# Second attention layer: query blocks take 3 to 9 ticks by their width, and low parts of the probabilities meet only V's high columns

## The chip, the cores and the metric

The kernel runs on one core of one Trainium2 chip. The metric is the device time of one execution in microseconds (us). Three runs of the kernel before took 1335.98, 1336.43 and 1338.58 us; the median is 1336.43.

## What is computed

Two layers over a sequence of 1024 tokens, width 1024, float32. Layer A is chunked attention with 16 heads of 64 and a learned bias. Then one shared K and V is projected from the stream. Layer B is differential attention against it: 8 heads, each with two softmax maps, the second subtracted from the first with a learned factor. Only layer B's attention is changed:

```python
s = jnp.einsum('bhmqd,bhmkd->bhmqk', qblk, k).astype(jnp.float32) * scale
qchunk = (bi * Q_BLOCK + jnp.arange(Q_BLOCK)) // CHUNK
mask = kchunk[None, :] <= qchunk[:, None]
s = jnp.where(mask[None, None, None], s, NEG_INF)
p = jax.nn.softmax(s, axis=-1)
a = p[:, :, 0] - lam * p[:, :, 1]
return jnp.einsum('bhqk,bhkd->bhqd', a.astype(v.dtype), v)
...
o = rmsnorm(o, b_subln[j]) * (1.0 - lam_init)
y = (o.reshape(B, S, B_WIDTH) * jax.nn.silu(g)) @ b_w_out[j]
```

The mask is causal, so query block i (128 tokens, i = 0 to 7) needs the key blocks 0 to i: its scores are 128 x 128(i + 1).

## The kernel before

**Numbers.** Every float32 operand of a matrix product is kept as a high and a low part (`hi_of` on ScalarE, L189, and `lo_of` on VectorE, L192), and a product is the sum of high x high, high x low and low x high. V stands as 128 high and 128 low columns side by side, so a matmul of a block of probabilities against it has 256 output columns; the two halves are added afterwards (L972 and L948).

**Order by ticks.** The class `Ticks` writes the program in the order in which the engines get it. In a tick come first the tensor operations registered for it with `K.at`, then four matmuls of a filler (the projections of the layer, a stream of 128x512 matmuls, L232 to L236), then what `K.after` and `K.later` registered for the other engines, by rank and then by the order of registering. Nothing is reordered at run time: each engine takes its instructions in that order and waits for what each one needs.

**Units.** A unit is one head of layer B: 48 ticks, 192 fillers. In this text the ticks of a unit's attention are counted from its block 0; its tick 48 is tick 0 of the next unit. While a unit's attention runs, the fillers compute its own V and gate projections in the ticks 0 to 23 and then K, Q, K, Q of the next unit (two token halves), six ticks a group; the four K and Q groups end with the ticks 29, 35, 41 and 47.

**A block** of `attB_block` starts at tick t0 with the scores of its first map (L562), and at t1 come those of the second. The scores of both go to one tile `sp` in PSUM, of which the pool `psS` has a single buffer: a matmul of scores waits until VectorE has read the ones before (the reduction, L571, emitted in the tick of the scores). ScalarE's exponential (L577) follows a tick later. Before, t1 = t0 + 3, and a block follows the last after 6 ticks. Counted from t1 the rest stands the same before and after:
- tick t1 + 2: `norm` on GpSimd, two inverses (L169) and a scaling (L901 before, L905 after);
- tick t1 + 3: `mix` on VectorE, which subtracts the second map from the first (L906, then L910);
- tick t1 + 5, for key blocks 4 to 7 also t1 + 6: the transposes of the mixed probabilities (L165), then high and low parts;
- four ticks after the transposes: the matmuls against V (L936, then L941). The block is closed seven ticks later with a transpose of its output (`c5`) and a product on VectorE (`c6`, L967, then L972).

**Rotation of K and Q** (`rope`). When a K or Q group ends, ScalarE copies it (L851), four small DMAs move pieces of it, GpSimd multiplies twice (L857, L858, emitted two and three ticks later), VectorE adds (L859, six ticks later), ScalarE makes the high parts (seven ticks) and VectorE the low parts (L192 on 64 partitions, twice, eight ticks later).

**Weights.** GpSimd scales a weight slice (L207, in the ticks 0, 18, 24 and 42 of a unit's attention), ScalarE makes its high part two ticks later and VectorE its low part (`wlo`) three ticks later.

Of the kernel before, what the change touches and what calls it, by code (L numbers as in the profile page):

```python
# [23 lines left out]
P = 128  # L24
# [27 lines left out]
def bcast_rows(ap, n):  # L52
    """[1, n] DRAM row -> the same row on every partition."""
    return ap.broadcast_to([P, n])


class Ticks:
    """Emission order: every tick issues its tensor work, a few filler matmuls,
    then the work of the other engines that is due."""
# [47 lines left out]
def trunk(ctx, tc, x, positions, a_norm_pre, a_w_in, a_rel_rev, a_w_out, a_norm_post,  # L107
# [27 lines left out]
    # DRAM scratch  # L135
# [8 lines left out]
    # resident operands  # L144
# [37 lines left out]
    def sumsq(src, dump):  # L182
        """row sums of squares; the squares themselves go to dump, which is free."""
        ss = st()
        A.activation(dump, src, AF.Square, accum_out=ss)
        return ss
# [7 lines left out]
    # ---------------------------------------------------------------- weights  # L194
# [17 lines left out]
    class Weights:  # L212
        """slices in the order of use; a slice's load goes out with the split before it."""
# [13 lines left out]
    def mm_group(w, xT):  # L227
        """one [128 cols, 512 tokens] projection, a matmul at a time."""
        hi, lo = w
        acc = acc_tile()  # L230
        for c in range(NC):
            T.matmul(acc, lhsT=hi[:, c, :], rhs=xT(0, c), start=(c == 0), stop=False)  # L232
            yield acc
            T.matmul(acc, lhsT=hi[:, c, :], rhs=xT(1, c), start=False, stop=False)  # L234
            yield acc
            T.matmul(acc, lhsT=lo[:, c, :], rhs=xT(0, c), start=False, stop=(c == NC - 1))  # L236
            yield acc
# [3 lines left out]
    def proj_stream(W, xT, done, slow, quarters=False):  # L241
        """every projection of a layer; kinds k, q, v, g are slices 0..3 of a unit."""
        seq = [(u, kind, half) for u in range(8) for kind, half in ORDER]
        if quarters:
            yield from mm_quarters(W, xT(0), done)
        for n, (u, kind, half) in enumerate(seq):
            if quarters and n < 2:
                continue
            m = 0
            for acc in mm_group(W.cut[4 * u + kind], xT(half)):  # L250
                m += 1
                if m == 2 and n + 1 < len(seq):
                    k = 4 * seq[n + 1][0] + seq[n + 1][1]
                    if k not in W.cut:
                        W.split(k)
                if m == 24:
                    done(u, kind, half, acc)
                yield
                if n >= 61 and m % slow == 0:
                    yield  # L260

    def mm_quarters(W, xT, done):
        """the first two groups, 256 tokens at a time."""
        accs = [acc_tile(), acc_tile()]
        for part in range(2):
            cs = slice(part * 256, part * 256 + 256)
            for kind in range(2):
                hi, lo = W.cut[kind]
                m = 0
                for c in range(NC):  # L270
                    for w, l in ((hi, 0), (hi, 1), (lo, 0)):
                        T.matmul(accs[kind][:, cs], lhsT=w[:, c, :], rhs=xT(l, c)[:, cs],
                                 start=(m == 0), stop=(m == 23))
                        m += 1
                        if m == 24 and part == 1:
                            done(0, kind, 0, accs[kind])
                        if m % 2 == 0:
                            yield

    # ------------------------------------------------------------ prologue  # L280
# [5 lines left out]
    # eight times the bias table, by distance  # L286
# [37 lines left out]
    # flag: 0 when the frames are consecutive  # L324
# [44 lines left out]
    # small constants of layer B  # L369
# [31 lines left out]
    # bias of layer A for consecutive frames  # L401
# [19 lines left out]
    # ---------------------------------------------------- normalised activations  # L421
    # chunk c of token half h in slot h*8 + c, hi then lo
# [7 lines left out]
    def transposed(u, cg, dst, spare=False):  # L430
        """four chunks of u [128 tokens, 1024] into dst(hi or lo, cg)."""
# [8 lines left out]
    def norm_in(t, k):  # L440
        """token tile t of layer A's input, from tick k."""
# [10 lines left out]
    # ------------------------------------------------------- layer A, attention  # L452
    # slots of R2 (layer A) and R1 (layer B): 0,1 Q half 0; 2,3 K even unit; 4,5 V even unit;
    #                8,9 Q half 1; 10,11 K odd unit; 12,13 V odd unit; 14,15 probabilities
# [23 lines left out]
    def split_q(src, qq, half, k):  # L478
        """[two heads x 64, 512] -> per head hi and lo, each on both partition halves."""
# [15 lines left out]
    def split_k(src, kt, k):  # L495
        """[two heads x 64, 512] -> per head hi on its own partition half, lo on the other."""
# [13 lines left out]
    def v_tokens(acc, view, hi, lo):  # L510
        """v^T in PSUM -> token rows, hi and lo."""
# [13 lines left out]
    def gate(acc, gl):  # L525
        """2 silu(g)."""
# [26 lines left out]
    def qk(qq, ks, head, i, j0):  # L553
        """scores of query block i against key blocks j0..i."""
# [12 lines left out]
    def scores(sp, add, w):  # L567
        """-(psum + add)/8 and its row minimum."""
# [11 lines left out]
    def attA(u, base):  # L580
        """registers the attention of a head pair from tick base: 6 ticks a (query pair, head)."""
        par = u % 2
        for sidx in range(8):
            pr, hh = sidx // 2, sidx % 2
            attA_pair(u, par, pr, hh, base + 6 * sidx)
# [111 lines left out]
    # ------------------------------------------------------- output projections  # L697
    def wout(view, R, n, k):
        """column half n as hi and lo in slots n*8 + c of R, from tick k (writes from k + 4)."""
# [14 lines left out]
    class OutTiles:  # L714
        """token tiles of the gated attention output, as hi and lo stationary operands."""
# [22 lines left out]
    def out_stream(O, R, gpost, res, dst, more):  # L738
        """output projection with its residual; tiles 0 and 1 go first with one column half each."""
# [26 lines left out]
    def scaled(y, g):  # L766
        """a column half of y: times g, and the sum of its squares."""
# [6 lines left out]
    def finish(t, first, second, h, dst, more):  # L774
        """h + rmsnorm(y) * gpost for a token tile; more(t, h) goes on with it."""
# [15 lines left out]
    # rotary tables, spread over the ticks of a unit  # L791
# [35 lines left out]
    # ------------------------------------------------------------ layer B  # L827
# [15 lines left out]
    def rope(acc, half, then):  # L843
        """rotated [128, 512] from PSUM; then(tile, ticks)."""
# [28 lines left out]

    def attB(u, base):
        par = u % 2
        for i in range(NT):
            attB_block(u, par, i, base + 6 * i)

    def attB_block(u, par, i, t0):
        w = (i + 1) * P  # L880
# [29 lines left out]
        part(1, t0 + 3)  # L910
        K.after(t0 + 5, norm)
        K.after(t0 + 6, mix, 1)
        nbat = (i + 4) // 4

        def batch(b, t):
# [13 lines left out]
            def av(pt):  # L929
# [4 lines left out]
                for k in range(nb):  # L934
                    for l in range(2):
                        T.matmul(acc, lhsT=pt[:, l, k * P:(k + 1) * P], rhs=vvB(par, b)[:, k, :],  # L936
# [41 lines left out]
        for b in range(nbat):  # L978
            batch(b, t0 + 8 + 1 * b)

    # -------------------------------------------------------------- the program
# [66 lines left out]
def general_bias(nc, tc, gp, positions, rel, bias_t):  # L1048
    """Bias of every head and query block for frames in any order."""
# [94 lines left out]
```

## Time and profile before

| | |
|---|---|
| runs, median of 3 | 1336.43 us (1335.98 to 1338.58) |
| span of the profiled execution, first to last instruction | 1333.5 us |
| the profiled execution's own time | not listed apart from its span |
| TensorE busy (matmuls) | 1294.4 us, 97% |
| VectorE busy | 837.0 us, 63% |
| ScalarE busy | 661.9 us, 50% |
| GpSimd busy | 601.4 us, 45% |
| granted TensorE clock, mean | 0.994 |

A span is counted inside one execution, a run's time from outside; the median of the runs is 2.9 us over the span. A matmul's busy time in the profile has a modelled end, and matmuls overlap, so what one costs is read from the distance of two starts. An idle time in brackets counts from the modelled end.

### The profile page before, as it was taken

To read this page: it belongs to the slowest core of one execution; us is meant where nothing else is said; L and a number is where in the kernel's file an instruction comes from. 1 tells how busy PE (TensorE), PEld (TensorE's weight loads), DVE (VectorE), ACT (ScalarE), POOL (GpSimd) and SP (SyncE) were. 2 spreads that over 40 slices of the span, in tenths; PEclk is the share of its full clock that TensorE was granted. 3 is DMA by queue.
4 is the path that set the end of the run, shared out by engine and by line. 5 is a ranking of instruction groups with operands and counts; after the bars stand their busy time and mean duration, and the time that the engine had idled before them with its cause. 6 is when DMAs were issued, how large, how long until landed. Compare 5 with 4: busy or idle time off the path is not lost.

```text
span 1333.5 us, 20510 instructions
## 1 busy us (share of the span) xinstructions
PE 1294.4 (97%) x6919; PEld 1091.2 (82%) x6919; DVE 837.0 (63%) x1584; ACT 661.9 (50%) x1462; POOL 601.4 (45%) x846
## 2 busy tenths in 40 slices
PE   5999999999999999999998999999999999999998
PEld 5888888888888888878876888888888888888886
DVE  5557756765564646664446776767676768588643
ACT  4344464465454545553334555555555555466311
POOL 2244534444444444432245565555464646464311
PEclk8999999999999999999999999999999999999999
DMA  6454545454545444643433121212121212115343
GB/s 214 121 169 114 155 130 160 117 147 130 150 119 143 124 134 114 205 158 108 135 120 94 46 64 41 73 44 73 47 72 44 76 43 77 43 51 181 99 155 102
DMA packets 142484, 146.33 MB, mean 110 GB/s; under 512 B 11904, under 2 KB 112288, under 8 KB 142368
## 3 DMA queue, kind: packets, MB, share of 16 engines
q1 hardware_dynamic: 74400, 104.52, 27.2%
q10 hardware_dynamic: 67968, 40.39, 10.2%
q8 instruction: 57, 0.93, 0.3%
q14 instruction: 59, 0.48, 0.1%
HBM read 102.91 MB, written 26.23 MB: 97 GB/s over the span
## 4 chain that ended last, share of the span: by engine, by line
PE 45%; POOL 4%; DVE 4%; issue 3%; DMA 1%; ACT 1%; SPq 1%; DVEq 0%; POOLq 0%; ACTq 0%
PE acc L748 12%; PE acc L236 7%; PE acc L232 7%; PE acc L234 7%; PE sp L562 5%; PE tp L165 4%; PE av L936 4%; DVE s L906 2%; DMA sw<-xs 1%; POOL st L169 1%; POOL sw L858 1%; POOL xs L857 1%; SPq L853 1%; DVE R L192 0%; DVE xs L859 0%
## 5 line engine op out<-in xcount | busy, mean ns | idle before, releaser
L236 PE MATMUL acc<-R,wlo 128*128 128x512 f32 x1008 | 411.4, 408 | 0.7 <-DVE wlo L192 0.7
L234 PE MATMUL acc<-R,whi 128*128 128x512 f32 x1008 | 403.6, 400 | 0.8 <-DVE R L192 0.8
L232 PE MATMUL acc<-R,whi 128*128 128x512 f32 x1008 | 402.4, 399 | 1.9 <-ACT whi L189 1.6
L169 POOL TENSOR_TENSOR st<-st,mone 128x1 f32<-128x1 f32 x256 | 166.5, 653 | 335.9 <-ACT s L577 332.0
L577 ACT ACTIVATE s<-s,st 128x640 f32<-128x640 f32 (+7 forms) x256 | 188.4, 736 | 132.7 <-DVE st L571 124.6
L192 DVE TENSOR_TENSOR R<-tp,R 128x512 fp32r<-128x512 f32 (+3 forms) x304 | 180.6, 603 | 116.9 <-ACT R L189 116.2
L189 ACT CAST R<-tp 128x512 fp32r<-128x512 f32 (+3 forms) x304 | 156.4, 516 | 158.3 <-PE tp L165 156.1
L236 PEld LDWEIGHTS acc<-R,wlo 128*128 128x128 f32 x1008 | 189.9, 188 | 35.8 <-DVE wlo L192 2.0
L234 PEld LDWEIGHTS acc<-R,whi 128*128 128x128 f32 x1008 | 190.2, 189 | 33.7 <-DVE R L192 1.1
L232 PEld LDWEIGHTS acc<-R,whi 128*128 128x128 f32 x1008 | 190.6, 189 | 31.5 <-ACT whi L189 2.1
L562 PE MATMUL sp<-R 128*128 128x256 f32 (+3 forms) x768 | 174.0, 335 | 3.6 <-DMA R<-R 3.1
L571 DVE CUSTOM_DVE_ANT_0 s<-sp,mask 128x256 f32<-128x256 f32 (+7 forms) x128 | 96.7, 755 | 124.0 <-PE sp L562 123.0
L748 PE MATMUL acc<-R,ohi 128*128 128x512 f32 x512 | 163.1, 398 | 0.0
L562 PEld LDWEIGHTS sp<-R 128*128 128x128 f32 x768 | 136.5, 189 | 25.3 <-issue 3.5
L571 DVE CUSTOM_DVE_ANT_0 s<-sp,bt 128x640 f32<-128x640 f32 (+4 forms) x128 | 83.9, 656 | 79.3 <-PE sp L562 48.3
L165 PEld LDWEIGHTS tp<-ident,s 128*128 128x128 f32 x768 | 97.5, 140 | 42.2 <-DVE s L906 10.3
L165 PE MATMUL tp<-ident,s 128*128 128x128 f32 x768 | 123.2, 272 | 7.6 <-DVE s L906 7.6
L748 PEld LDWEIGHTS acc<-R,ohi 128*128 128x128 f32 x512 | 95.2, 189 | 20.3
L616 POOL TENSOR_SCALAR s<-s,st 128x640 f32<-128x640 f32 (+4 forms) x128 | 105.6, 825 | 12.6
L748 PE MATMUL acc<-R,olo 128*128 128x512 f32 x256 | 103.2, 403 | 0.0
L664 PE MATMUL av<-R 128*128 128x256 f32 (+1 forms) x576 | 89.4, 277 | 3.5 <-ACT R L189 1.9
L664 PEld LDWEIGHTS av<-R 128*128 128x128 f32 x576 | 82.8, 191 | 8.8 <-ACT R L189 3.2
(123 smaller groups left out, 1619.2 us busy)
## 6 DMA issues: line engine op xcount, KB each, us to landing
bt<-bias_t SPq DMA_DIRECT2D x64, 320.0 KB
R<-R SPq DMA_DIRECT2D x64, 256.0 KB
wst<-in_a_w_in_dram ACTq DMA_DIRECT2D x29, 512.0 KB
wst<-in_kv_w_dram ACTq DMA_DIRECT2D x16, 512.0 KB
wst<-in_b_w_in_dram ACTq DMA_DIRECT2D x16, 512.0 KB
bias_t<-b SPq DMA_DIRECT2D x16, 320.0 KB
xt<-in_x_dram SPq DMA_DIRECT2D x8, 512.0 KB
bt<-bias_t SPq DMA_DIRECT2D x16, 256.0 KB
```

The costliest lines, as they stand in the source:

```text
L165: T.transpose(dst, src, ident)
L169: G.tensor_tensor(out=r, in0=a, in1=mone, op=ALU.pow)
L189: A.copy(out=hi, in_=src)
L192: V.tensor_tensor(out=lo, in0=src, in1=hi.bitcast(F32), op=ALU.subtract)
L232: T.matmul(acc, lhsT=hi[:, c, :], rhs=xT(0, c), start=(c == 0), stop=False)
L234: T.matmul(acc, lhsT=hi[:, c, :], rhs=xT(1, c), start=False, stop=False)
L236: T.matmul(acc, lhsT=lo[:, c, :], rhs=xT(0, c), start=False, stop=(c == NC - 1))
L562: T.matmul(sp[:, a:b], lhsT=q[:, l, (i % 4) * P:(i % 4 + 1) * P], rhs=ks[:, head, j0 * P + a - c0:j0 * P + b - c0], start=(l == 0), stop=( ...
L571: V.tensor_tensor_reduce(out=s[:, 0:w], in0=sp, in1=add, op0=ALU.add, op1=ALU.min, scale=-0.125, scalar=BIG, accum_out=mx)
L577: A.activation(s[:, 0:w], s[:, 0:w], AF.Exp, bias=mx, scale=-1.0, accum_out=sums)
L664: T.matmul(acc[:, o0:o0 + n], lhsT=vvA(par, j // 4)[:, j % 4, hh * P:(hh + 1) * P], rhs=pt[:, l, col:col + n], start=(first and l == 0), s ...
L748: T.matmul(y, lhsT=lhs[:, c, :], rhs=R[:, n * 8 + c, l * 512:(l + 1) * 512], start=(m == 0), stop=(m == 23))
```

## The change

`B_TICKS` gives the blocks 0 to 7 of a unit 3, 4, 5, 6, 6, 7, 8 and 9 ticks (48 as before), and t1 lies half of that, rounded up, behind t0. So t0 and t1 of the blocks are 0 and 2, 3 and 5, 7 and 10, 12 and 15, 18 and 21, 24 and 28, 31 and 35, 39 and 44; before, block 7 had 42 and 45. The second part of the change narrows the matmuls of the low parts of the probabilities from 256 to 128 columns: the product of the low parts of both operands is left out. Comments and docstrings go too; those lines are left out here.

```diff
+    B_TICKS = (3, 4, 5, 6, 6, 7, 8, 9)
+
     def attB(u, base):
         par = u % 2
         for i in range(NT):
-            attB_block(u, par, i, base + 6 * i)
+            attB_block(u, par, i, base + sum(B_TICKS[:i]))
 
     def attB_block(u, par, i, t0):
+        t1 = t0 + (B_TICKS[i] + 1) // 2
         w = (i + 1) * P
...
         part(0, t0)
-        part(1, t0 + 3)
-        K.after(t0 + 5, norm)
-        K.after(t0 + 6, mix, 1)
+        part(1, t1)
+        K.after(t1 + 2, norm)
+        K.after(t1 + 3, mix, 1)
         nbat = (i + 4) // 4
...
                 for k in range(nb):
                     for l in range(2):
-                        T.matmul(acc, lhsT=pt[:, l, k * P:(k + 1) * P], rhs=vvB(par, b)[:, k, :],
+                        n = 256 - l * P
+                        T.matmul(acc[:, 0:n], lhsT=pt[:, l, k * P:(k + 1) * P], rhs=vvB(par, b)[:, k, 0:n],
                                  start=(j0 + k == 0 and l == 0), stop=(j0 + k == i and l == 1))
...
         for b in range(nbat):
-            batch(b, t0 + 8 + 1 * b)
+            batch(b, t1 + 5 + b)
```

How the order moves is seen where block 7 of one unit meets block 0 of the next.

**GpSimd, block 7's `norm` (two L169 and a TENSOR_SCALAR).** Before:

```order
L207 TENSOR_TENSOR wst<-wst,kvg 128x1024
L857 TENSOR_TENSOR xs<-xs,cos 128x512
L858 TENSOR_TENSOR sw_8248<-sw_8248,sin 128x512
L178 TENSOR_SCALAR st<-st 128x1
L179 TENSOR_TENSOR st<-st,mhalf 128x1
L169 TENSOR_TENSOR st<-st,mone 128x1 x2
L901 TENSOR_SCALAR st<-st,nlam 128x1
L207 TENSOR_TENSOR wst<-wst,bng 128x1024
```

And now:

```order
L207 TENSOR_TENSOR wst<-wst,kvg 128x1024
L857 TENSOR_TENSOR xs<-xs,cos 128x512
L858 TENSOR_TENSOR sw_8248<-sw_8248,sin 128x512
L169 TENSOR_TENSOR st<-st,mone 128x1 x2
L905 TENSOR_SCALAR st<-st,nlam 128x1
L178 TENSOR_SCALAR st<-st 128x1
L179 TENSOR_TENSOR st<-st,mhalf 128x1
L207 TENSOR_TENSOR wst<-wst,bng 128x1024
```

The `norm` still stands behind both multiplies of the rotation; the two small operations of an earlier block have come between it and the scaling of the weights.

**VectorE, block 7's `mix` (the row of 128x1024 with the operands s and st).** Before:

```order
L192 TENSOR_TENSOR wlo<-wst,whi 128x1024
L192 TENSOR_TENSOR R_125<-tp,R_125 128x384
L859 TENSOR_TENSOR xs<-xs,sw_8248 128x512
L955 TENSOR_SCALAR tt<-tt,st 128x128
L571 ISA s,st<-sp,mask 128x128
L571 ISA st 128x1
L906 SCALAR_TENSOR_TENSOR s<-s,st 128x1024
L192 TENSOR_TENSOR R_125<-xs,R_125 64x512 x2
L948 SCALAR_TENSOR_TENSOR tt<-av,st,tt 128x128
L967 SCALAR_TENSOR_TENSOR ot<-tp,sub,g 128x256
L571 ISA s,st<-sp,mask 128x128
```

And now:

```order
L972 SCALAR_TENSOR_TENSOR ot<-tp,sub,g 128x256
L192 TENSOR_TENSOR wlo<-wst,whi 128x1024
L953 SCALAR_TENSOR_TENSOR tt<-av,st,tt 128x128
L910 SCALAR_TENSOR_TENSOR s<-s,st 128x1024
L859 TENSOR_TENSOR xs<-xs,sw_8248 128x512
L571 ISA s,st<-sp,mask 128x128
L571 ISA st 128x1
L192 TENSOR_TENSOR R_125<-xs,R_125 64x512 x2
L960 TENSOR_SCALAR tt<-tt,st 128x128
L571 ISA s,st<-sp,mask 128x128
```

The `mix` now stands ahead of the rotation's sum L859 and of block 0's first reduction; the second reduction of block 0 is the last row of both.

**TensorE, from block 7's second transposes to block 1's first scores (256 wide).** Before:

```order
L165 MATMUL tp<-ident,s 128x128 x4
L562 MATMUL sp<-R_125 128x128 x2
L232 MATMUL acc<-R_126,whi 128x512
...
L236 MATMUL acc<-R_126,wlo 128x512
L562 MATMUL sp<-R_125 128x256 x2
```

And now:

```order
L165 MATMUL tp<-ident,s 128x128 x4
L562 MATMUL sp<-R_125 128x128 x2
L236 MATMUL acc<-R_126,wlo 128x512
L232 MATMUL acc<-R_126,whi 128x512
L234 MATMUL acc<-R_126,whi 128x512
L236 MATMUL acc<-R_126,wlo 128x512
L562 MATMUL sp<-R_125 128x256 x2
```

Between block 0's second scores and block 1's first, which share the one `sp` buffer, twelve fillers stood before; now four do.

## Rows read from the trace of the kernel before

**Rows 1.** The page: the span, and busy time of the engines.

```profile
span 1333.5 us, 20510 instructions
...
PE 1294.4 (97%) x6919; PEld 1091.2 (82%) x6919; DVE 837.0 (63%) x1584; ACT 661.9 (50%) x1462; POOL 601.4 (45%) x846
```

**Rows 2.** Waits, 725 to 1260 us: engine, line <- releaser: total us, times, longest us.

```profile
DVE s L571 <- PE sp L562: 120.7, 88, 3.1
...
PE tp L165 <- DVE s L906: 6.5, 7, 1.4
```

**Rows 3.** Timeline, TensorE, last block of one unit: start us, us, instruction [idle before <-releaser].

```profile
1038.35 1.09 PE L562 MATMUL sp<-R 128*128 128x512 f32 x4
1039.28 1.11 PE L936 MATMUL av<-R 128*128 128x256 f32 x8
1040.23 0.40 PE L232 MATMUL acc<-R,whi 128*128 128x512 f32 x1
...
1042.57 0.60 PE L165 MATMUL tp<-ident,s 128*128 128x128 f32 x4
1043.01 0.27 PE L165 MATMUL tp<-ident,tt 128*128 128x128 f32 x1
...
1045.30 0.39 PE L232 MATMUL acc<-R,whi 128*128 128x512 f32 x1
...
1048.10 0.33 PE L562 MATMUL sp<-R 128*128 128x128 f32 x2
...
1049.28 0.39 PE L232 MATMUL acc<-R,whi 128*128 128x512 f32 x1
...
1051.63 0.39 PE L234 MATMUL acc<-R,whi 128*128 128x512 f32 x1
1052.78 0.66 PE L165 MATMUL tp<-ident,s 128*128 128x128 f32 x4 [0.76 <-DVE s L906]
```

**Rows 4.** Timeline, GpSimd, the same stretch.

```profile
1037.59 1.19 POOL L169 TENSOR_TENSOR st<-st,mone 128x1 f32<-128x1 f32 x2
1038.89 0.34 POOL L901 TENSOR_SCALAR st<-st,nlam 128x1 f32<-128x1 f32 x1
...
1043.60 1.29 POOL L857 TENSOR_TENSOR xs<-xs,cos 128x512 f32<-128x512 f32 x1 [2.52 <-ACT s L577]
1044.86 1.29 POOL L858 TENSOR_TENSOR sw<-sw,sin 128x512 f32<-128x512 f32 x1
...
1048.98 0.81 POOL L901 TENSOR_SCALAR st<-st,nlam 128x1 f32<-128x1 f32 x1
1049.75 1.89 POOL L207 TENSOR_TENSOR wst<-wst,bng 128x1024 f32<-128x1024 f32 x1
1053.55 1.76 POOL L857 TENSOR_TENSOR xs<-xs,cos 128x512 f32<-128x512 f32 x1 [1.91 <-DVE R L192]
```

**Rows 5.** Timeline, VectorE, the same stretch.

```profile
1047.25 1.22 DVE L192 TENSOR_TENSOR wlo<-wst,whi 128x1024 fp32r<-128x1024 f32 x1
...
1048.85 0.68 DVE L859 TENSOR_TENSOR xs<-xs,sw 128x512 f32<-128x512 f32 x1
1049.45 0.28 DVE L955 TENSOR_SCALAR tt<-tt,st 128x128 f32<-128x128 f32 x1
1049.66 0.28 DVE L571 CUSTOM_DVE_ANT_0 s<-sp,mask 128x128 f32<-128x128 f32 x1
...
1049.87 2.86 DVE L906 SCALAR_TENSOR_TENSOR s<-s,st 128x1024 f32<-128x1024 f32 x1
1052.76 1.41 DVE L192 TENSOR_TENSOR R<-xs,R 64x512 fp32r<-64x512 f32 x2
```

**Rows 6.** Groups by line and shape, VectorE, 1206 to 1260 us: count | busy, mean ns.

```profile
L906 DVE SCALAR_TENSOR_TENSOR s<-s,st 128x1024 f32<-128x1024 f32 x1 | 1.3, 1284 | 1.2 <-POOL st L901 1.2
```

**Rows 7.** Timeline, ScalarE, the stretch of rows 3.

```profile
1049.57 1.26 ACT L189 CAST R<-xs 64x512 fp32r<-64x512 f32 x2 [0.63 <-DVE xs L859]
```

**Rows 8.** Timeline, TensorE, the first block of layer B.

```profile
717.52 0.30 PE L165 MATMUL tp<-ident,s 128*128 128x128 f32 x1 [1.10 <-DVE s L906]
```

## The prediction

> **What bounds the kernel now.** The page comes first: TensorE is busy for 97% of the span, no other engine for over 63% [rows 1]. So time can only be won by giving TensorE less to do, or where it waits. The waits of layer B's attention come second, and they are few [rows 2]. TensorE waits for `mix` (L906) seven times, 6.5 us in all; the other row, 120.7 us, is VectorE waiting for scores, which costs nothing as long as VectorE is early. The timeline shows where the seven stand: at block 7 of a unit, once in each unit but the last [rows 3]. The last matmul before the wait starts at 1051.63 and is worth 0.23 us, the transposes start at 1052.78, so 0.92 us are lost. The bracket says 0.76 because its modelled end is 0.16 late; with that added seven times, 6.5 becomes 7.6 us, 1.1 a unit.
>
> The other engines' timelines say why `mix` is late. GpSimd starts L207 at 1049.75 for 1.89 us, VectorE starts `mix` at 1049.87 and takes 2.86 us [rows 4, 5]. Alone the same instruction takes 1.28 us [rows 6]. So a VectorE operation with two operands in SBUF and a GpSimd operation don't run side by side; the second waits for the first. The other order is there too: L857, 1.29 us elsewhere, takes 1.76 at 1053.55, when VectorE was busy with L192 [rows 4, 5], and L901 takes 0.81 for 0.34 beside L859.
>
> **What the change does, part by part.** The profiled execution's span is 1333.5 us, the median of the runs 1336.43; I add the changes in the span to the median.
>
> *Narrow matmuls.* 288 of the 576 matmuls against V fall from 256 to 128 columns. Eight of 256 go from 1039.28 to 1040.23, 0.119 us each [rows 3]. For 128 columns, two matmuls of scores and eight against V stand between 1048.10 and 1049.28: 1.18 - 0.95 = 0.23, or 0.115 each. A 128-column matmul thus costs nearly what a 256-column one does, since each brings a load of weights, and the gain is 288 x 0.004 = 1.2 us. If cost went by columns, it would be 288 x 0.06 = 17 us. Nothing is slower by it; no bound is below zero.
>
> The Trainium skill (TensorE: Matmul & The Clock Gate, "Back-to-back issue gap") gives a gap of 56 ns for an isolated matmul of 128 columns; by that the part would win 288 x 0.063 = 18 us, an estimate. The trace doesn't agree: 0.115 us.
>
> *Ticks by width, away from block 7.* The ticks of a unit stay 48, so the sum of TensorE's work stays. In the units no wait on `mix` stands at blocks 1 to 6, so there the new spacing has nothing to win. From t1 on the distances inside a block are as before.
>
> *Block 7's transposes.* They move from tick 50 to tick 49. I count from the start of tick 42 (1038.35 in rows 3), where the K group of the ticks 36 to 41 has just ended, and sum TensorE's work up to tick 49: 28 fillers of 0.233 us (twelve from 1045.30 to 1048.10) are 6.53, the second scores of block 7 0.93 (1038.35 to 1039.28), 14 matmuls against V 1.66, block 0's scores 0.23, a transpose 0.11 (four in 0.44 from 1042.57): 9.47 us [rows 3]. What the transposes wait for: the multiplies L857 and L858 of that K group begin 5.25 us after the mark (copy and DMAs, which the change doesn't touch) and end at 7.80; `norm` stands behind them on GpSimd and takes 1.64 (1037.59 to 1039.23), `mix` 1.28 [rows 4, 6]. Before, tick 50 came 13.5 us after the mark, and this chain had time to spare. Now it ends at 10.72, so TensorE waits for 1.25 us. There is a second term. The weights' low part `wlo`, 1.22 us [rows 5], now follows `c6`, which needs a transpose of tick 45; tick 45 starts 4.7 us after the mark. So `wlo` falls into the multiplies, between 5.25 and 7.80, and one of them waits for it. With its whole length the wait is 2.5 us. I take 2.5, because in every ordering of the three the operands meet; the low end is 1.25.
>
> *Block 1's first scores.* They move from tick 54 to tick 51, one tick after block 0's second scores, and need the only `sp` buffer. What is queued on VectorE between `mix` and the reduction that frees it is now L859 (0.68), block 0's first reduction (0.28), the K group's low parts (1.41 for two), a scaling (0.28) and the reduction itself (0.28) [rows 5]; ScalarE's high parts (0.63 each) stand between L859 and the low parts [rows 7]. From the end of `mix`: 0.68 + 1.26 for the high parts, 0.70 for the last low part, 0.28 and 0.35 are 3.3 us. TensorE does eight transposes (0.88), eight fillers (1.86) and 0.23 of scores meanwhile, 2.97. Alone that is a wait of 0.3 us. But L207 runs in this stretch, since two small operations now part it from `norm`, and holds up the low parts by up to its 1.89 us: 4.6 us, a wait of 1.65. And the next group's L857 comes due about 5 us after tick 48, three after `mix` starts: another 1.29 [rows 4], a wait of 2.95. I take 2.3, between the last two.
>
> *Sum of a boundary.* 2.5 + 2.3 = 4.8 us instead of 1.1, at seven boundaries: 7 x 3.7 = 25.9 us more.
>
> *The first block of layer B.* Its transposes wait 1.1 + 0.16 us for the same chain [rows 8]; they come a tick of fillers earlier, 0.93 us, while the chain stays: 0.9 more.
>
> *L207 at the ticks 18 and 24* now meets the `mix` of the blocks 3 and 4, where it met that of the blocks 2 and 3. These transposes come two ticks after their `mix`, 1.9 us of fillers and other work, which hides up to 1.6 us of delay; I cost it at nothing, and at 0.5 us for each of 16 at most, 8 us, if VectorE is late already.
>
> Together: 1336.4 + 25.9 + 0.9 - 1.2 = **1362.0 us**. With the upper end of both waits (2.5 + 2.95) it is 1366.6, and with most of the 8 us at the blocks 3 and 4, 1373.
>
> **Rivals.**
> 1. *The engines just miss each other.* `wlo` runs ahead of the multiplies, and L207 and L857 fall behind the low parts. Then a boundary costs 1.25 + 0.3 instead of 1.1: 7 x 0.45 + 0.9 - 1.2 = 2.9, or 1339.3 us. For it: the small operations between `norm` and L207 take `mix` out of L207's way. Against it: `wlo`'s place behind the transpose of tick 45.
> 2. *Faster: block 7's wait goes.* The second scores come a tick earlier, at 44, so `mix` may too, with L207 no longer ahead of it. If the chain reaches `mix` 1.25 us before my 9.44, the 7.6 us vanish: 1336.4 - 7.6 - 1.2 = 1327.6. It decides at L858's end, 6.5 us after the mark instead of 7.8; the DMAs and two multiplies of 1.29 speak against that.
> 3. *Columns count.* The narrow matmuls save 17 us, for the load of weights hides behind the wide one beside it. With the waits, 1362.0 - 15.9 = 1346.1. Against it: 0.115 us above.
>
> **How the numbers follow.** The forecast gets 0.70, the first rival 0.15, the second 0.09, the third 0.06. A measurement of this kernel can tell about 0.2%, 2.7 us, from no change: 1333.8 to 1339.1 is the same. The first rival lies on its upper edge, so it is shared between same (0.09) and slower (0.06). Faster 0.09, same 0.09, slower 0.82. The range reaches from 1338, which takes in most of the first rival, to 1373; about 0.18 is left out.
>
> **What would show it.** Right, if after's timeline has at each boundary two waits of TensorE, one at block 7's transposes for `mix` (about 2.5 us, before 0.9) and one at block 1's first scores for L571 (about 2.3, before none), if L858 ends nearly 8 us after tick 42 or later, and if a pair of 256 and 128 columns takes 0.23 us. Wrong, if the waits at block 7 are under 1 us, if block 1's scores don't wait, or if such a pair takes under 0.2 us.

## The result, and the profile after

| | before | after |
|---|---|---|
| runs, median | 1336.43 us (1335.82 to 1339.2) | 1389.88 us (1385.92 to 1390.11) |
| span of the profiled execution | 1333.5 us | 1388.2 us |
| mean granted TensorE clock | 0.994 | 0.980 |

After over before is 1.0386, with a 95% interval from 1.037 to 1.0402: 53 us slower. The forecast had the sign and the two waits right and was half the size, and 1389.88 lies above the range. The page of after, to be held against [rows 1]:

```profile
span 1388.2 us, 20495 instructions
...
PE 1316.1 (95%) x6919; PEld 1099.0 (79%) x6919; DVE 863.1 (62%) x1584; ACT 659.0 (47%) x1462; POOL 603.5 (43%) x846
```

TensorE issues the same 6919 matmuls, is busy longer, and a smaller share of a longer span: it waits, and some matmuls run slower. The view of the waits of TensorE in layer B (725 to 1340 us; engine, line and releaser, then total us, times, longest) tells the first half. L910 is `mix`, L906 before; [rows 2] had 6.5 us and no wait of scores:

```profile
PE tp L165 <- DVE s L910: 23.4, 19, 3.0
PE sp L562 <- DVE st L571: 12.2, 7, 2.9
PE tp L165 <- DVE tt L960: 1.8, 1, 1.8
```

One boundary (the third), TensorE's timeline, which answers to [rows 3]. Columns: start us, us, instruction, [idle before <- releaser].

```profile
916.61 0.39 PE L232 MATMUL acc<-R,whi 128*128 128x512 f32 x1
...
919.40 1.03 PE L941 MATMUL av<-R 128*128 128x256 f32 x8
920.27 0.45 PE L236 MATMUL acc<-R,wlo 128*128 128x512 f32 x1
920.56 0.40 PE L232 MATMUL acc<-R,whi 128*128 128x512 f32 x1
...
928.15 0.66 PE L165 MATMUL tp<-ident,s 128*128 128x128 f32 x4 [1.96 <-DVE s L910]
...
929.94 0.42 PE L562 MATMUL sp<-R 128*128 128x128 f32 x2
...
933.20 0.50 PE L562 MATMUL sp<-R 128*128 128x256 f32 x2 [1.85 <-DVE st L571]
```

Tick 42 starts with the filler at 916.61, eight fillers ahead of block 7's second scores. Both forecast waits are there, at block 7's transposes (928.15) and at block 1's first scores (933.20). The eight matmuls against V and one filler take 920.56 - 919.40 = 1.16 us; less the filler's 0.233 that is 0.93, for 0.95 before.

GpSimd and VectorE in the same stretch, to be held against [rows 4, 5]:

```profile
921.76 1.29 POOL L857 TENSOR_TENSOR xs<-xs,cos 128x512 f32<-128x512 f32 x1 [2.86 <-DMA sw<-xs]
923.00 1.30 POOL L858 TENSOR_TENSOR sw<-sw,sin 128x512 f32<-128x512 f32 x1
924.26 2.05 POOL L169 TENSOR_TENSOR st<-st,mone 128x1 f32<-128x1 f32 x2
926.41 0.34 POOL L905 TENSOR_SCALAR st<-st,nlam 128x1 f32<-128x1 f32 x1
...
928.48 1.98 POOL L207 TENSOR_TENSOR wst<-wst,bng 128x1024 f32<-128x1024 f32 x1
931.32 1.53 POOL L857 TENSOR_TENSOR xs<-xs,cos 128x512 f32<-128x512 f32 x1 [0.87 <-DMA sw<-xs]
```

```profile
923.12 2.26 DVE L192 TENSOR_TENSOR wlo<-wst,whi 128x1024 fp32r<-128x1024 f32 x1
925.30 0.34 DVE L953 SCALAR_TENSOR_TENSOR tt<-av,st,tt 128x128 f32<-128x128 f32 x1
926.79 1.30 DVE L910 SCALAR_TENSOR_TENSOR s<-s,st 128x1024 f32<-128x1024 f32 x1 [1.15 <-POOL st L905]
...
929.39 2.33 DVE L192 TENSOR_TENSOR R<-xs,R 64x512 fp32r<-64x512 f32 x2 [0.48 <-ACT R L189]
931.75 1.18 DVE L960 TENSOR_SCALAR tt<-tt,st 128x128 f32<-128x128 f32 x1
932.85 0.28 DVE L571 CUSTOM_DVE_ANT_0 s<-sp,mask 128x128 f32<-128x128 f32 x1
```

From the start of L857 to the end of `mix` it is 928.09 - 921.76 = 6.33 us; the working had 6.72 with `wlo` between the multiplies at its full price, 5.47 without. `wlo` is there (923.12); it waits for L858's end, and the two small L169 of `norm` behind wait for `wlo`. So it is at four of the seven boundaries, where the first L169 takes 1.53 us for 0.55; at the other three `wlo` is ahead of L858, which takes 2.28 for 1.30. Either way it costs 0.98 us. Then `mix` runs alone, 1.30 us. Behind it the K group's low parts take 2.33 us beside L207, for 1.41 in [rows 5], and a scaling takes 1.18 beside L857: both end late, and the reduction that frees `sp` ends at 933.13.

What no step of the prediction had is in a view of windows: a stretch, its length, busy time of PE, PEld, DVE, ACT and POOL with the instructions, then the granted clock (1.00 is 2.4 GHz, 0.50 is 1.2 GHz), DMA share and GB/s.

```profile
929.00:933.20 4.20, 2.35 (x15) 1.63 (x13) 3.75 (x6) 3.40 (x8) 3.33 (x3) 1.00 0.09 20
934.10:937.50 3.40, 3.40 (x13) 2.72 (x11) 1.92 (x5) 0.60 (x2) 2.41 (x4) 0.50 0.02 5
937.50:941.00 3.50, 3.50 (x24) 3.11 (x23) 1.18 (x4) 1.37 (x5) 0.00 (x0) 1.00 0.00 0
```

Behind the two waits TensorE's clock falls to half for 3.4 us, in which it does 13 matmuls for 24 in the next 3.5. There are seven such stretches at the boundaries (one of them 6.8 us) and two in the last unit, where before had none. The view shows where they stand and not what sets them off.

I add up what TensorE loses in layer B, as the distance between the starts of two matmuls over what the first is worth (0.457 ns a column, 0.110 us at least):

| lost time of TensorE, us | before | after | more | predicted |
|---|---|---|---|---|
| block 7's transposes, wait for `mix` | 8.1 | 17.2 | +9.1 | +9.8 |
| block 1's first scores, wait for L571 | 0 | 13.9 | +13.9 | +16.1 |
| half clock behind these waits | 0 | 11.1 | +11.1 | not priced |
| last unit (waits 9.6, half clock 3.8) | 0.6 | 13.4 | +12.8 | not priced |
| transposes of blocks 3 to 5, wait for `mix` | 0.1 | 7.0 | +6.9 | 0, bound 8 |
| start of layer B | | | +1.9 | +0.9 |
| matmuls against V | | | -2.0 | -1.2 |

The sum is 53.7 us; the spans differ by 54.7. The last row is not measured: it is the 288 narrowed matmuls at the difference of the two worths, 0.007 us each. The waits at block 1's scores differ widely, from 0.5 to 3.0 us.

### The profile page after: what moved, and what is told of

The parts are those of the page before. It is cut to its first block, busy times and chain, and to the rows that moved or that the text cites. A ratio compares the mean times of both kernels' runs of the same rounds, so it can differ in the third digit from the quotient of the medians.

```text
span 1388.2 us, 20495 instructions
## 1 busy us (share of the span) xinstructions
PE 1316.1 (95%) x6919; PEld 1099.0 (79%) x6919; DVE 863.1 (62%) x1584; ACT 659.0 (47%) x1462; POOL 603.5 (43%) x846
## 4 chain that ended last, share of the span: by engine, by line
PE 39%; DVE 7%; POOL 5%; issue 4%; ACT 3%; DMA 1%; SPq 1%; ACTq 0%; DVEq 0%; POOLq 0%
PE acc L748 11%; PE acc L236 6%; PE acc L232 6%; PE acc L234 6%; PE sp L562 4%; PE av L941 3%; PE tp L165 3%; DVE R L192 2%; POOL st L169 2%; DVE s L910 2%; DMA sw<-xs 1%; ACT s L577 1%; POOL sw L858 1%; ACT R L189 1%; DVE s L571 1%
## 5 line engine op out<-in xcount | busy, mean ns | idle before, releaser
L232 PE MATMUL acc<-R,whi 128*128 128x512 f32 x1008 | 410.0, 407 | 1.9 <-ACT whi L189 1.6
L234 PE MATMUL acc<-R,whi 128*128 128x512 f32 x1008 | 410.3, 407 | 0.8 <-DVE R L192 0.8
L169 POOL TENSOR_TENSOR st<-st,mone 128x1 f32<-128x1 f32 x256 | 162.5, 637 | 392.5 <-ACT s L577 381.9
L234 PEld LDWEIGHTS acc<-R,whi 128*128 128x128 f32 x1008 | 192.9, 191 | 34.6 <-DVE R L192 1.1
L232 PEld LDWEIGHTS acc<-R,whi 128*128 128x128 f32 x1008 | 192.8, 191 | 32.8 <-ACT whi L189 2.1
L562 PE MATMUL sp<-R 128*128 128x256 f32 (+3 forms) x768 | 176.7, 339 | 15.9 <-DVE st L571 12.8
L571 DVE CUSTOM_DVE_ANT_0 s<-sp,mask 128x256 f32<-128x256 f32 (+7 forms) x128 | 96.8, 756 | 112.0 <-PE sp L562 111.5
L748 PE MATMUL acc<-R,ohi 128*128 128x512 f32 x512 | 165.4, 403 | 0.0
L165 PE MATMUL tp<-ident,s 128*128 128x128 f32 x768 | 126.6, 278 | 25.2 <-DVE s L910 24.2
L571 DVE CUSTOM_DVE_ANT_0 s<-sp,bt 128x640 f32<-128x640 f32 (+4 forms) x128 | 84.1, 657 | 80.7 <-PE sp L562 50.2
L748 PEld LDWEIGHTS acc<-R,ohi 128*128 128x128 f32 x512 | 96.4, 191 | 20.9
L748 PE MATMUL acc<-R,olo 128*128 128x512 f32 x256 | 103.9, 406 | 0.8 <-DVE olo L192 0.8
L192 DVE TENSOR_TENSOR wlo<-wst,whi 128x1024 fp32r<-128x1024 f32 x64 | 84.9, 1326 | 8.8 <-POOL sw L839 4.3
```

Source lines behind the costliest of these rows:

```text
L165: T.transpose(dst, src, ident)
L169: G.tensor_tensor(out=r, in0=a, in1=mone, op=ALU.pow)
L192: V.tensor_tensor(out=lo, in0=src, in1=hi.bitcast(F32), op=ALU.subtract)
L562: T.matmul(sp[:, a:b], lhsT=q[:, l, (i % 4) * P:(i % 4 + 1) * P], rhs=ks[:, head, j0 * P + a - c0:j0 * P + b - c0], start=(l == 0), stop=( ...
L571: V.tensor_tensor_reduce(out=s[:, 0:w], in0=sp, in1=add, op0=ALU.add, op1=ALU.min, scale=-0.125, scalar=BIG, accum_out=mx)
L748: T.matmul(y, lhsT=lhs[:, c, :], rhs=R[:, n * 8 + c, l * 512:(l + 1) * 512], start=(m == 0), stop=(m == 23))
```

## The experiments

Each run is told as its median and its ratio to the kernel before, with the 95% interval. Lost time is counted as in the table above. Lines shift by a few where an edit adds some.

**The two halves of the change.** First the new ticks with the matmuls of before:

```diff
-                        n = 256 - l * P
-                        T.matmul(acc[:, 0:n], lhsT=pt[:, l, k * P:(k + 1) * P], rhs=vvB(par, b)[:, k, 0:n],
+                        T.matmul(acc, lhsT=pt[:, l, k * P:(k + 1) * P], rhs=vvB(par, b)[:, k, :],
```

> The new ticks with all matmuls against V 256 wide again. My theory: the ticks make the whole loss and narrow matmuls are worth 1 to 2 us, so 1391 us (1389 to 1393), with both waits at each boundary as in the changed kernel (2.4 us at block 7's transposes, 2 us at block 1's scores). Rival, columns count: the wide ones cost 17 us more, 1405 to 1407. Rival, the narrow matmuls themselves shorten the cover and make part of the loss: under 1385.

Measured: 1389.33 us, 1.0393 (1.037 to 1.0415). The waits are those of after (17.4 us at block 7, 16.1 at block 1, half clock 10). Then the reverse, the old ticks with the narrow matmuls, the same lines put into the kernel before:

> Six ticks for every block as before, low parts of the probabilities against V's high columns alone (the product of both low parts is left out). My theory: a 128-column matmul costs nearly what a 256-column one does, 1334.5 to 1335.5 us, 1 to 2 us under the kernel before, and a pair of 256 and 128 columns takes 0.23 us. Rival, columns count: 1319 to 1321.

Measured: 1335.39 us, 0.9998 (0.9987 to 1.001). The ticks make the whole loss, and 288 matmuls of half the width gain nothing that can be measured: the interval has room for 1.2 us (0.0009) and none for 17 (0.013). The third rival, that columns count, falls.

**Block 1's first scores.** The prediction put this wait down to VectorE's queue between `mix` and the reduction. Two edits try it. The first takes the low parts of the second K half out of that queue:

```diff
-    def split_k(src, kt, k):
+    def split_k(src, kt, k, wait=0):
...
-        K.later(k + 1, lo)
+        K.later(k + 1 + wait, lo)
...
-            rope(acc, half, lambda xs, k: split_k(xs, ksB(par)[:, :, half * 512:half * 512 + 512], k))
+            rope(acc, half, lambda xs, k: split_k(xs, ksB(par)[:, :, half * 512:half * 512 + 512], k, 2 * half))
```

> The changed kernel with the low parts of the second K half two ticks later, behind block 0's second reduction on VectorE. My theory: block 1's first scores wait because that reduction stands behind those low parts; their wait (13.9 us over seven boundaries) falls to 1 to 3 and part of the half clock at the boundaries (11 us) goes with it: 1370 to 1378 us; the wait of block 7's transposes stays at 17 us. Rival, the reduction is late for another reason (VectorE as a whole is behind): the wait stays, 1388 to 1392.

Measured: 1369.96 us, 1.0239 (1.0223 to 1.0254). The wait is gone, 13.9 us to nothing; block 7's stays (17.7), and so does most of the half clock (9.3). VectorE's and TensorE's timelines at the same boundary:

```profile
928.03 1.71 DVE L960 TENSOR_SCALAR tt<-tt,st 128x128 f32<-128x128 f32 x1
930.61 0.29 DVE L571 CUSTOM_DVE_ANT_0 s<-sp,mask 128x128 f32<-128x128 f32 x1 [0.87 <-PE sp L562]
```

```profile
931.96 0.40 PE L562 MATMUL sp<-R 128*128 128x256 f32 x2
932.20 0.40 PE L232 MATMUL acc<-R,whi 128*128 128x512 f32 x1
```

Now VectorE waits for the scores (0.87 us), not TensorE for VectorE. The second edit leaves the queue and aims at the single `sp` buffer: blocks 0 to 3 write their two heads' scores into two halves of one `sp` tile.

```diff
+    def qk_narrow(head, par, i):
+        if (i, head) == (0, 0):
+            spn[0] = psS.tile([P, 1024], F32, tag="sp", name="sp")
+        q, w = qqB(0, head), (i + 1) * P
+        out = spn[0][:, 512 * head:512 * head + w]
...
-                cell["sp"] = qk(qqB, ksB(par), m, i, 0)
+                cell["sp"] = qk_narrow(m, par, i) if i < 4 else qk(qqB, ksB(par), m, i, 0)
```

> The changed kernel, but blocks 0 to 3 of a unit put the scores of their two maps into two halves of one tile, so that block 1's first scores wait for block 0's first reduction and no longer for its second. My theory: the 13.9 us at block 1's scores go, and with only one wait left at a boundary most of the slices at half clock (11 us) too: 1365 to 1376 us. Rival, VectorE is simply behind there and the wait turns up at the next use (high and low parts, matmuls against V): 1385 to 1390.

Measured: 1387.45 us, 1.0369 (1.0352 to 1.0386); the wait stays, 18.3 us. VectorE's and TensorE's timelines:

```profile
933.46 0.28 DVE L571 CUSTOM_DVE_ANT_0 s<-sp,mask 128x128 f32<-128x128 f32 x1
```

```profile
933.80 0.80 PE L885 MATMUL sp<-R 128*128 128x256 f32 x2 [2.82 <-DVE st L571]
```

Block 1's scores still start right behind the second reduction of block 0, though they go to the other half. The dependency seems to be kept for the tile and not for its halves, so the edit did not free the buffer and tries neither expectation; whether a second buffer would help is open.

**Block 7's transposes.** In the prediction the multiplies L857 and L858 of the second K half stand ahead of `norm`. Here those of the second half alone (`late`) are put behind it, at the seventh tick instead of the second and third, and all that follows them five ticks later:

```diff
-        K.later(2, lambda: G.tensor_tensor(out=xs, in0=xs, in1=rot["cos"][:, cs], op=ALU.mult))
-        K.later(3, lambda: G.tensor_tensor(out=w, in0=w, in1=rot["sin"][:, cs], op=ALU.mult))
-        K.later(6, lambda: V.tensor_tensor(out=xs, in0=xs, in1=w, op=ALU.add))
-        then(xs, 6 + 1)
+        K.later(7 if late else 2, lambda: G.tensor_tensor(out=xs, in0=xs, in1=rot["cos"][:, cs], op=ALU.mult))
+        K.later(7 if late else 3, lambda: G.tensor_tensor(out=w, in0=w, in1=rot["sin"][:, cs], op=ALU.mult))
+        K.later(11 if late else 6, lambda: V.tensor_tensor(out=xs, in0=xs, in1=w, op=ALU.add))
+        then(xs, (11 if late else 6) + 1)
```

> The changed kernel with both multiplies of the second K half behind block 7's norm on GpSimd, and its sum, high and low parts five ticks later. My theory: block 7's transposes wait because norm stands behind those multiplies; their wait falls from 17 us to 4 to 8, that of block 1's scores to under 3, and the half clock at the boundaries to under 3: 1357 to 1364 us. Rival, the exponentials of block 7 are late by themselves: the wait of the transposes stays over 14 us, 1370 to 1376.

Measured: 1370.3 us, 1.0242 (1.0227 to 1.0258), a miss. Block 7's wait falls from 17.2 to 4.1 us, block 1's scores no longer wait, and the half clock at the boundaries is gone. But 11.2 us now go to block 0's transposes and 8.3 to block 1's. GpSimd's timeline shows why:

```profile
925.10 1.30 POOL L857 TENSOR_TENSOR xs<-xs,cos 128x512 f32<-128x512 f32 x1
926.37 1.29 POOL L858 TENSOR_TENSOR sw<-sw,sin 128x512 f32<-128x512 f32 x1
927.63 2.26 POOL L857 TENSOR_TENSOR xs<-xs,cos 128x512 f32<-128x512 f32 x1
929.85 1.73 POOL L858 TENSOR_TENSOR sw<-sw,sin 128x512 f32<-128x512 f32 x1
931.54 0.55 POOL L169 TENSOR_TENSOR st<-st,mone 128x1 f32<-128x1 f32 x1
```

Two pairs of multiplies stand together, 6.5 us, and the `norm` of the next unit's blocks waits behind them. The edit shows that the multiplies held block 7's chain, and that the wait moves with them.

**L207 beside `mix`.** The prediction costed this meeting at nothing. L207 in two halves of 512 elements lets `mix` in between:

```diff
-            G.tensor_tensor(out=w, in0=w, in1=gain.unsqueeze(2).broadcast_to([P, NC, P]), op=ALU.mult)
+            for c in range(0, NC, 4):
+                G.tensor_tensor(out=w[:, c:c + 4, :], in0=w[:, c:c + 4, :],
+                                in1=gain[:, c:c + 4].unsqueeze(2).broadcast_to([P, 4, P]), op=ALU.mult)
```

> The changed kernel with the scaling of a weight slice on GpSimd in two halves of 512 elements a partition instead of one of 1024. My theory: the waits at the transposes of the blocks 3 to 5 (7 us) are mixes held up by that scaling, and so is a part of block 1's wait; a held-up operation waits for 0.95 us at most instead of 1.9: 1377 to 1384 us. Rival, VectorE is short of time in these ticks whatever GpSimd does: 1388 to 1391, and the waits at blocks 3 to 5 stay.

Measured: 1369.64 us, 1.0242 (1.0227 to 1.0258). In after, block 3 of a unit looks so in the timeline of all engines:

```profile
882.23 1.90 POOL L207 TENSOR_TENSOR wst<-wst,kvg 128x1024 f32<-128x1024 f32 x1
882.30 2.37 DVE L910 SCALAR_TENSOR_TENSOR s<-s,st 128x512 f32<-128x512 f32 x1
...
884.82 0.41 PE L165 MATMUL tp<-ident,s 128*128 128x128 f32 x2 [0.41 <-DVE s L910]
```

With halves the same `mix` takes 1.51 us, and the waits of blocks 3 and 4 go from 5.9 us to nothing. Most of the rest is block 1's wait (13.9 to 11.0) and the half clock at the boundaries (11.1 to 4.6): more than expected, because the clock's part was not in the expectation.

Before, the same two operations met at block 3 and no transpose waited. There `norm` ended (875.58) while VectorE still had a reduction ahead of `mix`, so that L207 had run for 1.0 us when `mix` started, and `mix` took 1.41:

```profile
875.54 1.90 POOL L207 TENSOR_TENSOR wst<-wst,bng 128x1024 f32<-128x1024 f32 x1
876.57 1.41 DVE L906 SCALAR_TENSOR_TENSOR s<-s,st 128x512 f32<-128x512 f32 x1
```

In after `norm` ends at 882.27, behind the reduction, and sets both going at once: L207 stands next to it on GpSimd, and `mix` needs its result. Block 4's `mix` starts 0.7 us behind L207 and takes 1.86 for 0.88. It is so in all seven units with an L207 there. The same edit as above, L207 in halves, in the kernel before, with its old ticks and its full matmuls:

> The kernel before with L207 in two halves of 512 elements. Theory (block 7's wait of before is mix held up by L207 whole: 1.28 us alone, 2.86 beside it): a half holds mix for about 0.95 instead of 1.6 us, so most of the 8 us of waits at block 7 go: 1329 to 1332 us. Rival (in the order of before the multiplies L857 and L858 and norm end mix's chain, and halves change nothing): 1334 to 1338 us, the wait of about 0.9 us at block 7 stays.

Measured: 1329.74 us (1328.57 to 1332.6), 0.9951 (0.9938 to 0.9964). It beats both kernels. The timeline of all engines at the boundary of [rows 3]:

```profile
1044.59 3.02 POOL L208 TENSOR_TENSOR wst<-wst,bng 128x512 f32<-128x512 f32 x2
...
1044.71 2.00 DVE L908 SCALAR_TENSOR_TENSOR s<-s,st 128x1024 f32<-128x1024 f32 x1
...
1046.76 0.44 PE L165 MATMUL tp<-ident,s 128*128 128x128 f32 x2
```

`mix` takes 2.00 us for 2.86, the transposes hardly wait (8.1 us became 2.1 over all units). So in the kernel before, the wait at block 7 was `mix` held up by L207.

**The last unit** has no next unit's groups of K and Q. The changed kernel with six ticks per block in that unit alone:

```diff
-            attB_block(u, par, i, base + sum(B_TICKS[:i]))
+            attB_block(u, par, i, base + sum(tk[:i]), tk[i])
...
+        tk = B_TICKS if u < 7 else (6,) * NT
```

> The changed kernel with six ticks for every block of the last unit alone. My theory: the last unit has fewer fillers in a tick, wide blocks of output weights on VectorE and small blocks packed into the first ticks; its 13 us of waits and half clock fall to about 1: 1376 to 1380 us. Rival, the last unit loses whatever its ticks are: 1388 to 1390.

Measured: 1373.74 us, 1.0276 (1.026 to 1.0291): 16 us back, more than expected. Part of the surplus stands at the boundary into the unit, where the wait of 3.0 us for scores and the 6.8 us at half clock are gone; a transpose there waits 2.0 us instead. The unit loses 13.4 us in after; its longest single waits are those of block 7's transposes, 2.1 us, and of a transpose behind the scaling L960:

```profile
1315.53 0.33 PE L165 MATMUL tp<-ident,tt 128*128 128x128 f32 x1 [1.81 <-DVE tt L960]
```

**Block 7's chain alone, a tick earlier, in the old order** (with the narrow matmuls, which cost nothing): the second scores, `norm` and `mix` of block 7 one tick earlier, the transposes where they were.

```diff
-        part(1, t0 + 3)
-        K.after(t0 + 5, norm)
-        K.after(t0 + 6, mix, 1)
+        t1 = t0 + (2 if i == 7 else 3)
+        part(1, t1)
+        K.after(t1 + 2, norm)
+        K.after(t1 + 3, mix, 1)
```

> Six ticks for every block, the narrow matmuls, and in block 7 alone the second scores, norm and mix a tick earlier while its transposes stay where they were. My theory: the wait of block 7's transposes in the kernel before (8 us) is mix held up by the scaling of weights; with the chain a tick earlier mix comes ahead of it and the wait goes: 1326 to 1329 us. Rival, norm is held by the multiplies of the K group, so that mix is no earlier: 1333 to 1337.

Measured: 1342.03 us, 1.0037 (1.0024 to 1.0049). Both expectations miss. Block 7's wait falls only from 8.1 to 6.1, and small new ones come in (2.1 us at transposes of `tt`, 1.8 at matmuls against V, and 2.7 of half clock at the start of layer B, which other runs have too). GpSimd's and VectorE's rows at the boundary of [rows 3] show why `mix` is not free:

```profile
1051.56 1.90 POOL L207 TENSOR_TENSOR wst<-wst,bng 128x1024 f32<-128x1024 f32 x1
1051.64 2.90 DVE L906 SCALAR_TENSOR_TENSOR s<-s,st 128x1024 f32<-128x1024 f32 x1 [1.66 <-POOL st L901]
```

An earlier `norm` brings L207 forward as well, for it stands right behind it, and both start together again.

**Do the terms add up?** The changed kernel with three of the edits: the low parts two ticks later, the last unit even, L207 in halves.

> The changed kernel with the three edits together that were worth 16, 20 and 20 us alone: six ticks per block in the last unit, the low parts of the second K half two ticks later, L207 in halves. Theory (three separate waits, with a part of the half clock shared by two of them): 1389.9 - 16 - 20 - 20 = 1334, and up to 8 us more for the half clock that two of them would each have won back: 1334 to 1342 us, no wait at block 1's first scores, about 1.5 us a boundary left at block 7's transposes. Rival (the same engines stay short of time and the waits move on): over 1350 us.

Measured: 1353.67 us, 1.0131 (1.0115 to 1.0146): 36 us back where they gave 20, 16 and 20 alone. All of what is left stands in one place: block 7's transposes wait 17.1 us in all, and behind them the clock falls at every boundary, 11.0 us. Part of the missing 20 us had been counted twice: the halves had won 2.9 us of block 1's wait, which the later low parts win too. And the 6.5 us of half clock that the halves had won alone are not won here: with one wait of 2.2 to 2.8 us left at each boundary the half clock comes back whole. The rest was not taken apart. So the next edit goes for that wait: `wlo` of the K and V groups ahead of block 7's second reduction, out of the multiplies.

```diff
-            K.later(2, lambda: hi_of(w, hi))
-            K.later(3, lambda: lo_of(w, hi, lo), 2)
+            early = gain is kvg
+            K.later(2, lambda: hi_of(w, hi), -2 if early else 1)
+            K.later(2 if early else 3, lambda: lo_of(w, hi, lo), -1 if early else 2)
```

> The run with three edits together, and the weights' low part wlo of the K and V groups before block 7's second reduction instead of behind c6, so that it ends before the multiplies begin. Theory (the prediction's second term: wlo between the multiplies holds up L858, 2.29 us instead of 1.29, and with it norm and mix): the reduction comes 1.2 us later, which the chain has room for; mix starts 0.9 to 1.4 us sooner, block 7's wait falls from 2.4 to between 1.0 and 1.5 us, 7 to 10 us less, and what TensorE loses at half clock goes in part: 1336 to 1347 us. Rival (the second reduction, its exponential and norm take the place of L858 at the end of the chain): the wait stays at 2 us or more, 1350 to 1357 us.

Measured: 1338.9 us, 1.0018 (1.0008 to 1.0028): another 15 us back, and 51 of the 53 in all. The timeline of all engines at the third boundary:

```profile
910.14 1.23 DVE L192 TENSOR_TENSOR wlo<-wst,whi 128x1024 fp32r<-128x1024 f32 x1
...
913.31 1.28 POOL L861 TENSOR_TENSOR sw<-sw,sin 128x512 f32<-128x512 f32 x1
...
914.56 1.06 POOL L169 TENSOR_TENSOR st<-st,mone 128x1 f32<-128x1 f32 x2
...
916.10 1.30 DVE L914 SCALAR_TENSOR_TENSOR s<-s,st 128x1024 f32<-128x1024 f32 x1 [2.93 <-POOL st L909]
...
917.46 0.66 PE L165 MATMUL tp<-ident,s 128*128 128x128 f32 x4 [2.10 <-DVE s L914]
```

`wlo` is out by 911.37, and the small L169 take 1.06 us for 2.05. Block 7's wait is 11.9 us in all: 1.5 to 1.8 at six boundaries, 2.3 at this one, and 1.7 in the mean, over the 1.0 to 1.5 expected. Only behind this one does the clock fall, so 9.4 of the 15 us are half clock. Last, the same with block 7's transposes a tick later, `t1 + 6` for `t1 + 5`:

> The same with block 7's transposes a tick later, at tick 50, where they stood before the change. Theory: another tick of four fillers, 0.93 us, covers what is left of the wait, no half clock is left, and the time is that of the kernel before without its own wait at block 7, 1328 to 1334 us: then the widths' ticks cost nothing in themselves, only where the pieces meet. Rival (block 0 and block 1 of the next unit come on top of block 7's matmuls, and a new wait takes the place): over 1338 us.

Measured: 1345.58 us, 1.0067 (1.0054 to 1.008), a miss. Its waits of TensorE, 725 to 1340 us:

```profile
PE tp L165 <- DVE s L914: 7.1, 13, 1.0
PE acc L239 <- DVE wlo L192: 3.1, 5, 0.9
PE sp L565 <- DVE st L574: 0.6, 4, 0.2
```

Block 7's wait falls to 5.2 us and no half clock is left at the boundaries, but block 0's transposes wait 5.1 (0.8 without the tick), weights' low parts 4.5, scores 2.2. The waits named come to 17.0 us, where the run without the tick had 14.3 with its half clock; the profiled spans differ by about as much (1342.7 and 1340.2), the medians by 6.7, of which the rest is in neither trace. The wait moved on: the rival was right.

## Why the prediction was right in sign and short by half

**Right: the two waits of a boundary.** Block 7's transposes wait 2.4 us in the mean (2.5 forecast), block 1's first scores 2.0 (2.3 forecast). L858 ends 7.7 us after the start of tick 42 (916.61 to 924.30; 7.80 forecast), so the second rival, which needed 6.5, falls. The first term's parts hold: the multiplies ahead of `norm` (moved away, the wait falls by 13 us) and `wlo` among them, though at four boundaries it holds `norm` and not a multiply, and `wlo` out of the way gives 0.74 us a boundary, (17.1 - 11.9) / 7, where its whole 1.25 was added. The second term's choice, between L207 alone (1.65) and L207 with L857 (2.95), is what the timeline shows: both meet VectorE. That the mean came so near is partly luck, for the single waits go from 0.5 to 3.0. The first block's term holds as well: its transposes start 10.92 us after the layer's first scores (707.13 to 718.05), 10.83 before, with four fillers less ahead of them, so the chain stayed and 1.0 us is lost for 0.9. The first rival, that the engines just miss each other, had 1339.3 and falls.

**Right: the narrow matmuls.** Old ticks with narrow matmuls measure 0.9998 times before (0.9987 to 1.001): 1.2 us could not be seen, and the 17 us of the third rival could, and are not there. The Trainium skill (TensorE: Matmul & The Clock Gate, "Back-to-back issue gap") would have given 18 us, an estimate from its 56 ns for an isolated matmul, which by the section itself leaves the load of weights out; no run here agrees with it for these matmuls, each of which brings its own load.

**Wrong: "L207 at the ticks 18 and 24 ... I cost it at nothing".** It costs 6.9 us, near the bound of 8. `mix` of block 3, 512 columns, takes 2.37 us, where one of twice the width takes 1.28 alone [rows 6] and the same width 0.75 in the last unit, and the two ticks of cover do not hold it. The step took the meeting to be the one of before, moved on by a block. But before, L207 was half done when `mix` came, and now both start together, so `mix` waits for nearly all of it. Halves take the wait of blocks 3 and 4 to nothing.

**Wrong: nothing was priced for the last unit.** The step "at seven boundaries" left the eighth block 7 out. There the chain of a block runs against fillers of another kind (L748), and the unit loses 12.8 us more than before, 2.2 of them at that block 7; with even ticks in it, 16 us come back. Which operations hold up its other blocks was not taken apart.

**Wrong: a wait was taken to cost its own length.** Behind the waits the granted clock falls to 0.50 for 3.4 us, in which a matmul of 512 columns takes 0.43 us for 0.234, so some 1.5 us are lost each time: 11.1 us at the boundaries, 3.8 in the last unit (counted in it above). The step "Sum of a boundary" was 4.8 - 1.1 = 3.7 us; with the clock it measures 3.3 + 1.6 = 4.9. The kernel before had only shorter waits there, 0.9 to 1.5 us, and kept the clock at 1.00. No run tries the clock by itself, and what decides whether it falls stays open (last section).

Together 6.9 + 12.8 + 11.1 = 30.8 us, against a miss of 27.9; the boundary waits were forecast 2.9 us too long, which is the difference; the two small terms nearly cancel (+1.0 and -0.8).

## What to carry to other kernels

When steps are moved in a schedule where two engines exclude each other, list every place where their operations now meet, and look which of the two comes first and by how much: what stands right behind `norm` on GpSimd starts together with what `norm` releases on VectorE. Price a meeting at up to the longer one's whole length where a consumer follows within two ticks, and count the units without successors too. A wait of the main engine can cost more than its length when its clock falls behind it; first look whether the trace has waits of that size already, and what the clock did there. Splitting the long operation of the engine with time to spare (L207 in halves) was worth more than any order of the ticks tried here: 1329.74 us against 1336.43.

## What was not expected of the hardware

- **The clock falls behind waits that are short beside the work.** In the run with three edits there were seven waits of 2.2 to 2.8 us, and with each the granted clock fell to 0.50 for 3.4 us, at most 0.6 us from the wait's end. With `wlo` early, it did so with one wait of 2.3 us and with none of six of 1.5 to 1.8. But in the changed kernel with L207 in halves it fell at three boundaries of seven; at the other four, waits of 2.1 to 2.7 us, each with another of 1.9 behind it, left the clock at 1.00. So the length of a wait alone does not decide. The longest of them, TensorE's timeline and the view of windows:

```profile
921.32 0.66 PE L165 MATMUL tp<-ident,s 128*128 128x128 f32 x4 [2.43 <-DVE s L912]
```

```profile
921.40:924.80 3.40, 3.10 (x18) 2.35 (x18) 2.86 (x6) 2.76 (x6) 3.40 (x4) 1.00 0.04 7
```

- **Operations with one operand in SBUF wait too.** The scaling L960 takes 0.28 us in [rows 5] (L955 there) and 1.18 beside L857, 1.71 in the run with the low parts later. The prediction spoke of two operands only. The Trainium skill (SBUF — State Buffer, "Who interferes with whom") counts `tensor_scalar`, which this is, among those that can take the pair of ports shared with GpSimd when its operands meet the conditions; the trace agrees, by 0.28 and 1.18 us.
- **GpSimd's smallest operations wait for VectorE.** Two inverses of 128x1 take 2.05 us beside `wlo` and 1.06 without it, and these stand in the chain of `norm`.
